# The streamed weights' pool laid out first in SBUF, the constants and x behind it

## The chip, the core and the metric

One core of a Trainium2 chip runs the whole kernel. The metric is device time in microseconds for one execution, the median of the runs; a run is one launch.

## The reference, cut to what matters

One hybrid layer on x of 256 tokens by 2048 channels. All projections come from one large matrix, then four branches are made, gated, projected and summed, and a last projection and a layer norm follow:

```python
h = einsum('bsd,de->bse', x, w_in) + b_in          # 2048 -> 18048 columns
... = split(h, ...)                                # a, b, c, d branches and merge_logits
# a: gated linear recurrence; b: dilated attention, 12 heads; c: RWKV-7 scan; d: 31-tap convolution
for n in range(4):
    mixed += sigmoid(merge[:, :, n]) * ((ys[n] * silu(gates[n])) @ w_br[n])
out = layernorm(ALPHA * x + mixed @ w_out)
```

Almost all the arithmetic is in three matrices: w_in (2048 x 18048), w_br (four of 512 x 2048) and w_out (2048 x 2048), in float32, and each is read from HBM once.

## The kernel before, in words

Every weight passes through `split` (L196 to L204): a piece of 128 partitions x 1024 float32 numbers (two k-tiles of 512 columns) is loaded into a buffer `raw`, ScalarE casts it to the rounded format into `wh`, and VectorE writes the rest, `raw - wh`, into `wl`. x is split in the same way, once, at the start, into `xh` and `xl`, which stay. A product is then three matmuls: high x high, low x high, high x low. The buffers come from the pool `wp`: four of `raw`, three of `wh`, three of `wl`, of 4096 bytes in each partition.

Three loops use the pieces:

- `channel_major` (matmul in L229) has the weights as stationary operand, 128 columns of `wh` or `wl`, and moves 256 tokens past them. The moving operand is `xh`/`xl` for w_in, and `yah`/`yal`, `ych`/`ycl`, ... (the gated branch outputs, here called y) for w_br. A piece makes 24 matmuls.
- `token_major` (matmul in L248) has the tokens as stationary operand (`xh`/`xl` for the attention's V columns of w_in, `mh`/`ml` for w_out, 128 tokens each) and moves 512 columns of `wh`/`wl` past them (256 in w_out's fourth part).
- The last 256 columns of w_out (L974) lie in `lasth`/`lastl`, which take the place of `xh`/`xl`; the stationary operand is `mh`/`ml`.

Every matmul loads a stationary operand of its own, 128 columns, while the matmul before it runs. The small stages of the branches (generators, advanced by `pump` between the pieces) lie between these loops, in a program order that the framework's scheduler sets; two of them, L366 and L406, are sums over partitions with the constant `sums` as stationary operand and `sh`/`sl` moving, 256 columns.

Pools are laid out in SBUF in the order in which they are opened. The order before is: a block of 16512 bytes that the framework holds, `cp` (the constants, x), `wp` (the streamed weights), `bp` (everything else). A tile's size is rounded up to 32 bytes. All addresses here are bytes within each partition.

Of the kernel before, what the change touches and what calls it, by code (L numbers as in the profile page):

```python
# [75 lines left out]
def tile_hybrid(  # L76
# [4 lines left out]
    S, G, PE = nc.scalar, nc.gpsimd, nc.tensor  # L81
    V = Paced(tc, nc.vector)

    cp = ctx.enter_context(tc.tile_pool(name="cp", bufs=1))
    wp = ctx.enter_context(tc.tile_pool(name="wp", bufs=1))
    bp = ctx.enter_context(tc.tile_pool(name="bp", bufs=1))
    pss = ctx.enter_context(tc.tile_pool(name="pss", bufs=4, space=PSUM))
    psb = ctx.enter_context(tc.tile_pool(name="psb", bufs=4, space=PSUM))
# [973 lines left out]
```

## Time and profile before

| | |
|---|---|
| median of three runs | 1069.24 us (1069.06 to 1070.82) |
| the profiled execution | 1071.35 us, span 1069.6 us, granted clock 0.993 |
| busy, of the span | PE 98%, PEld 94%, DVE 66%, ACT 47%, POOL 4% |
| moved by DMA | 199.14 MB, mean 186 GB/s |

PE is TensorE's matmuls, PEld its weight loads, DVE VectorE, ACT ScalarE. The end of a matmul is modelled in these records, and matmuls overlap, so the duration of one (some 280 ns) is not what one costs; the time from the start of one to the start of the next is. The chain of waits merges equal neighbours, so its pieces of "x192" with a start and a length give that time as a quotient.

### The profile page before, as it was taken

To read this page: it belongs to the slowest core of one execution; us is meant where nothing else is said; L and a number is where in the kernel's file an instruction comes from. 1 tells how busy PE (TensorE), PEld (TensorE's weight loads), DVE (VectorE), ACT (ScalarE), POOL (GpSimd) and SP (SyncE) were. 2 spreads that over 40 slices of the span, in tenths; PEclk is the share of its full clock that TensorE was granted. 3 is DMA by queue.
4 is the path that set the end of the run, shared out by engine and by line. 5 is a ranking of instruction groups with operands and counts; after the bars stand their busy time and mean duration, and the time that the engine had idled before them with its cause. 6 is when DMAs were issued, how large, how long until landed. Compare 5 with 4: busy or idle time off the path is not lost.

```text
span 1069.6 us, 20338 instructions
## 1 busy us (share of the span) xinstructions
PE 1049.8 (98%) x8547; PEld 1008.0 (94%) x8547; DVE 707.6 (66%) x999; ACT 502.7 (47%) x621; POOL 39.3 (4%) x61
## 2 busy tenths in 40 slices
PE   9999999999999999999999999999999999999994
PEld 7999999989999989999999998899999999998884
DVE  6879989889769955575444444566665555556666
ACT  3474445666544435345444443346544444444342
POOL 0100000000110020000000000000000000000003
PEclk9999999999999999999999999999999999999997
DMA  9866666555576674458766666655456666766552
GB/s 309 256 208 180 197 185 181 168 165 158 176 191 179 188 196 139 149 152 263 216 182 193 182 192 181 190 166 155 130 169 195 184 191 202 211 201 210 191 188 79
DMA packets 106765, 199.14 MB, mean 186 GB/s; under 512 B 8036, under 2 KB 17024, under 8 KB 106672
## 3 DMA queue, kind: packets, MB, share of 16 engines
q1 hardware_dynamic: 102432, 185.62, 58.5%
q0 software_dynamic: 3520, 11.09, 3.6%
q8 instruction: 67, 1.10, 0.4%
q10 hardware_dynamic: 720, 1.11, 0.3%
q14 instruction: 26, 0.21, 0.1%
HBM read 194.77 MB, written 5.39 MB: 187 GB/s over the span
## 4 chain that ended last, share of the span: by engine, by line
PE 88%; DVE 6%; DMA 2%; issue 1%; ACT 1%; POOL 0%; SPq 0%; ACTq 0%
PE ps L229 69%; PE ps L248 13%; DVE wl L67 2%; DVE xw L67 2%; DMA raw<-in_w_in 1%; DVE z L67 1%; DMA x<-scr 1%; PE psl L769 1%; PE ps L974 1%; PE po L793 0%; POOL xt L600 0%; ACT wh L202 0%; ACT z L953 0%; PE py L706 0%; PE pab L550 0%
## 5 line engine op out<-in xcount | busy, mean ns | idle before, releaser
L67 DVE TENSOR_TENSOR wl<-raw,wh 128x1024 fp32r<-128x1024 f32 (+1 forms) x343 | 418.3, 1221 | 305.4 <-ACT wh L202 302.9
L202 ACT CAST wh<-raw 128x1024 fp32r<-128x1024 f32 (+1 forms) x343 | 359.0, 1048 | 488.5 <-PE ps L229 360.7
L229 PE MATMUL ps<-xh,wh 128*128 128x256 f32 x2064 | 580.0, 282 | 0.8 <-ACT wh L202 0.8
L229 PE MATMUL ps<-xl,wh 128*128 128x256 f32 x2064 | 577.7, 281 | 0.0
L229 PE MATMUL ps<-xh,wl 128*128 128x256 f32 x2064 | 574.4, 282 | 0.9 <-DVE wl L67 0.7
L229 PEld LDWEIGHTS ps<-xh,wh 128*128 128x128 f32 x2064 | 389.5, 189 | 3.1 <-ACT wh L202 2.0
L229 PEld LDWEIGHTS ps<-xl,wh 128*128 128x128 f32 x2064 | 389.7, 189 | 0.3
L229 PEld LDWEIGHTS ps<-xh,wl 128*128 128x128 f32 x2064 | 386.4, 189 | 3.3 <-DVE wl L67 2.0
L67 DVE SCALAR_TENSOR_TENSOR acc<-cu,pkt,acc 128x256 f32<-128x256 f32 x120 | 50.7, 483 | 0.0
L248 PE MATMUL ps<-wh,ml 128*128 128x512 f32 (+1 forms) x128 | 46.3, 363 | 0.0
L248 PE MATMUL ps<-wh,mh 128*128 128x512 f32 (+1 forms) x128 | 46.3, 363 | 0.0
L248 PE MATMUL ps<-wl,mh 128*128 128x512 f32 (+1 forms) x128 | 42.3, 362 | 0.0
L248 PE MATMUL ps<-wh,xh 128*128 128x512 f32 x96 | 38.1, 396 | 0.0
L248 PE MATMUL ps<-wh,xl 128*128 128x512 f32 x96 | 37.9, 395 | 0.0
L248 PE MATMUL ps<-wl,xh 128*128 128x512 f32 x96 | 34.6, 396 | 0.0
L811 ACT ACTIVATE mg<-ps,bc 128x256 f32<-128x256 f32 x64 | 26.8, 471 | 6.7 <-PE ps L229 6.6
L248 PEld LDWEIGHTS ps<-wh,ml 128*128 128x128 f32 x128 | 24.2, 189 | 3.8
L248 PEld LDWEIGHTS ps<-wh,mh 128*128 128x128 f32 x128 | 24.2, 189 | 3.7
L248 PEld LDWEIGHTS ps<-wl,mh 128*128 128x128 f32 x128 | 24.0, 189 | 3.7
L248 PEld LDWEIGHTS ps<-wl,xh 128*128 128x128 f32 x96 | 18.0, 188 | 4.4
L248 PEld LDWEIGHTS ps<-wh,xh 128*128 128x128 f32 x96 | 18.0, 188 | 4.2
L248 PEld LDWEIGHTS ps<-wh,xl 128*128 128x128 f32 x96 | 18.0, 188 | 4.2
(310 smaller groups left out, 989.7 us busy)
## 6 DMA issues: line engine op xcount, KB each, us to landing
raw<-in_w_in SPq DMA_DIRECT2D x281, 512.0 KB, 3.8
raw<-in_w_br SPq DMA_DIRECT2D x32, 512.0 KB, 4.1
raw<-in_w_out SPq DMA_DIRECT2D x32, 512.0 KB, 4.7
fscr<-frow POOLq DMA_DIRECT2D x3, 768.0 KB, 8.3
z<-in_x POOLq DMA_DIRECT2D x4, 512.0 KB, 5.3
xs<-in_x_t SPq DMA_DIRECT2D x7, 256.0 KB, 6.2
hb<-fscr POOLq DMA_DIRECT2D x3, 512.0 KB, 5.8
lng<-in_ln_g POOLq DMA_DIRECT2D x2, 512.0 KB, 6.1
```

The costliest lines, as they stand in the source:

```text
L67: ins = f(*a, **k)
L202: S.copy(h, raw)
L229: PE.matmul(o, w[:, k, j * P : (j + 1) * P], r[:, kk, :], start=(kk == 0 and i == 0 and j % 2 == 0), stop=(kk == nk - 1 and i == 2), skip_ ...
L248: PE.matmul(ps[t][:, 0:n], a(kk, t), w[:, k, :], start=(kk == 0 and i == 0), stop=(kk == KT - 1 and i == 2),)
L769: PE.matmul(ps[:, 0:w], qt[g][:, h, q * P : (q + 1) * P], kt[g][:, h, 0:w], start=True, stop=True)
L811: S.activation(g, ps[j], AF.Sigmoid, bias=bcol(c0 + j * P))
L974: PE.matmul(ps[:, 0:T], mix(a)(k, t), w[:, k, :], start=(k == 0 and i == 0), stop=(k == KT - 1 and i == 2))
```

## The change

Two lines that open pools change places:

```diff
-    cp = ctx.enter_context(tc.tile_pool(name="cp", bufs=1))
     wp = ctx.enter_context(tc.tile_pool(name="wp", bufs=1))
+    cp = ctx.enter_context(tc.tile_pool(name="cp", bufs=1))
     bp = ctx.enter_context(tc.tile_pool(name="bp", bufs=1))
```

On all five engines the built program holds the same instructions in the same order with the same waits (8006 rows on PE, 888 on DVE, 617 on ACT, 63 on POOL, 372 on SP, buffer numbers kept); what differs is the addresses of two pools. `wp` is 40960 bytes long and goes down by 45408; `cp` goes up by 40960; `bp` stays. First addresses in the two built programs, with the remainder to 64 and to 512:

| tile | before | mod 64 | mod 512 | after | mod 64 | mod 512 |
|---|---|---|---|---|---|---|
| `raw`, first of 4 | 61920 | 32 | 480 | 16512 | 0 | 128 |
| `wh`, first of 3 | 78304 | 32 | 480 | 32896 | 0 | 128 |
| `wl`, first of 3 | 90592 | 32 | 480 | 45184 | 0 | 128 |
| `xh` (and `lasth`) | 17536 | 0 | 128 | 58496 | 0 | 128 |
| `xl` (and `lastl`) | 33920 | 0 | 128 | 74880 | 0 | 128 |
| `sums` | 53056 | 0 | 320 | 94016 | 0 | 320 |
| y (`yah`, `ych`, ...) | 216032 | 32 | 480 | 216032 | 32 | 480 |
| `mh`, `ml`, `sh`, `sl` (one each) | 140256 | 32 | 480 | 140256 | 32 | 480 |

A stationary operand is 512 bytes of such a tile in each partition and a moving one 1024 or 2048, and both start at multiples of 512 from its first address, so the remainders hold for all of them.

## Rows read from the trace of the kernel before

**Rows 1.** The page's busy times, and the granted clock in 40 slices.
```profile
PE 1049.8 (98%) x8547; PEld 1008.0 (94%) x8547; DVE 707.6 (66%) x999; ACT 502.7 (47%) x621; POOL 39.3 (4%) x61
PEclk9999999999999999999999999999999999999997
```

**Rows 2.** The page's chain of waits, by line.
```profile
PE ps L229 69%; PE ps L248 13%; DVE wl L67 2%; DVE xw L67 2%; DMA raw<-in_w_in 1%; DVE z L67 1%; DMA x<-scr 1%; PE psl L769 1%; PE ps L974 1%; PE po L793 0%; POOL xt L600 0%; ACT wh L202 0%; ACT z L953 0%; PE py L706 0%; PE pab L550 0%
```

**Rows 3.** What PE waited for longest: us in total, times, longest.
```profile
PE pp L609 <- DMA x<-scr: 2.5, 1, 2.5
```

**Rows 4.** Groups of matmuls by line and shape: count, busy us, mean ns, idle.
```profile
L229 PE MATMUL ps<-xh,wh 128*128 128x256 f32 x2064 | 580.0, 282 | 0.8 <-ACT wh L202 0.8
L229 PE MATMUL ps<-xh,wl 128*128 128x256 f32 x2064 | 574.4, 282 | 0.9 <-DVE wl L67 0.7
...
L229 PE MATMUL ps<-ych,wh 128*128 128x256 f32 x64 | 18.1, 282 | 0.0
L248 PE MATMUL ps<-wh,xh 128*128 128x512 f32 x96 | 38.1, 396 | 0.0
...
L248 PE MATMUL ps<-wh,mh 128*128 128x256 f32 x32 | 9.0, 283 | 0.0
```

**Rows 5.** L229's matmuls by stretch: us, PE busy (count), clock, DMA share, GB/s.
```profile
0.00:240.00 240.00, 224.10 (x1857) 1.00 0.69 206
240.00:480.00 240.00, 210.82 (x1708) 0.99 0.59 169
...
306.85:352.00 45.15, 45.08 (x384) 1.00 0.63 180
```

**Rows 6.** The chain's pieces in two stretches with x moving: start, us, what.
```profile
129.91 35.13 PE ps L229 x296
...
479.97 145.14 PE ps L229 x1237
```

**Rows 7.** The chain, 797 to 826 us: x moving, then y moving.
```profile
797.41 22.54 PE ps L229 x192
...
819.95 5.74 PE ps L229 x48
```

**Rows 8.** Matmuls in order of time: 1st and 11th of eleven neighbours, y moving.
```profile
850.08 0.28 PE L229 MATMUL ps<-ych,wh 128*128 128x256 f32 x1
...
851.28 0.28 PE L229 MATMUL ps<-ycl,wh 128*128 128x256 f32 x1
```

**Rows 9.** The chain in token-major stretches: x, then m stationary (512, 256), then L974.
```profile
654.96 40.13 PE ps L248 x172
...
969.81 60.29 PE ps L248 x266
...
1039.66 5.26 PE ps L248 x44
...
1044.92 4.83 PE ps L974 x41
```

**Rows 10.** Matmuls in order of time: first and last of seven neighbours, `sums` stationary.
```profile
197.28 0.28 PE L366 MATMUL psm<-sl,sums 128*128 128x256 f32 x1
...
197.98 0.28 PE L366 MATMUL psm<-sl,sums 128*128 128x256 f32 x1
```

**Rows 11.** Groups of the casts and subtractions, whole pieces, on DVE and ACT.
```profile
L67 DVE TENSOR_TENSOR wl<-raw,wh 128x1024 fp32r<-128x1024 f32 x341 | 416.9, 1224 | 304.1 <-ACT wh L202 301.7 <-PE pst L783 1.4
L67 DVE TENSOR_TENSOR lastl<-raw,lasth 128x1024 fp32r<-128x1024 f32 x4 | 4.9, 1224 | 2.0 <-ACT lasth L968 2.0
...
L202 ACT CAST wh<-raw 128x1024 fp32r<-128x1024 f32 x341 | 357.8, 1050 | 484.7 <-PE ps L229 360.7 <-PE ps L248 76.3 <-issue 15.3
L968 ACT CAST lasth<-raw 128x1024 fp32r<-128x1024 f32 x4 | 4.2, 1050 | 5.4 <-DMA raw<-in_w_out 5.4
```

**Rows 12.** The chain, 309 to 390 us, by line.
```profile
by line: DVE wl L67 28.0%; DVE xw L67 23.5%; issue 14.4%; PE ps L229 13.7%; DMA x<-scr 9.5%; POOL xt L600 5.5%; DVE gd L67 2.9%; DVE mixed L67 2.1%; DVE mg L67 1.7%; ACT wh L202 1.3%; POOL x L601 0.8%; DVE ydl L67 0.1%
```

**Rows 13.** The longest piece of the chain's start.
```profile
13.35 7.51 DMA raw<-in_w_in
```

More of the change, by code (lines that the diff above doesn't have):

```diff
@@ L82, in tile_hybrid @@
     V = Paced(tc, nc.vector)
+    wp = ctx.enter_context(tc.tile_pool(name="wp", bufs=1))
     cp = ctx.enter_context(tc.tile_pool(name="cp", bufs=1))
-    wp = ctx.enter_context(tc.tile_pool(name="wp", bufs=1))
     bp = ctx.enter_context(tc.tile_pool(name="bp", bufs=1))
```

## The prediction

> **What bounds the kernel now.** I read the page's busy times first, then the chain, then PE's own waits. PE is busy over 98% of the span, and its granted clock is full (the 2.4 GHz level) in 39 of 40 slices, 7 tenths in the last [rows 1]. The chain lies 69% on the matmuls of L229 and 13% on those of L248 [rows 2]. PE's longest wait is 2.5 us, once, near 389 us [rows 3], and its waits in L229 for `wh` and `wl` come to 0.8 and 0.7 us [rows 4]. So the time is a count of matmuls times what one costs, plus a start and an end of some 20 us. L229 has 3 x 2064 matmuls with x moving and twelve groups of 64, that is 768, with y moving; L248 has three groups of 96 with x stationary (512 columns), three of 96 with m stationary (512), three of 32 with m stationary (256) [rows 4].
>
> Since no instruction moves, only the spacing of matmuls, the speed of ACT and DVE on the moved tiles, and the loads into `raw` can change. So I look for rows in which the same form of instruction meets different addresses.
>
> **What addresses do to a matmul before.** I call *distance* the address of the moving operand less that of the stationary one, to the modulus 512. In the two token-major stretches shape and type agree, and only tiles differ: with x stationary 40.13 us / 172 = 233.3 ns each, with m stationary 60.29 / 266 = 226.7 [rows 9]. The first is distance 480 - 128 = 352, the second 480 - 480 = 0. At 256 columns with m stationary: 5.26 / 44 = 119.5 with `wh`/`wl` moving (distance 0), 4.83 / 41 = 117.8 with `lasth`/`lastl` moving (distance 128 - 480, that is 160) [rows 9]. And in L229, where stretches of x and y alternate: x moving 22.54 / 192 = 117.4 (distance 160), y moving 5.74 / 48 = 119.6 (distance 0) [rows 7]. In the steady part of a y stretch ten steps take 1.20 us, 120.0 each [rows 8]; a stretch's first matmuls are a little closer, which makes 119.6 of 120.0 in 48. Three pairs, and in each the two streams' addresses go with the spacing. I conclude that a matmul's reads and the next one's weight load disturb each other, by their addresses.
>
> Is it the distance, or each operand's own place? At L366 `sums` is stationary and `sl`/`sh` move: distance 480 - 320 = 160, but with the moving tile at 32 mod 64 and the stationary at 0, the reverse of x's pair. Six steps take 0.70 us, 117 each [rows 10], x's spacing. So two pairs at one distance, in opposite places, cost the same. I take the distance as what counts, from 8 matmuls only; this is the weakest step.
>
> The Trainium skill, SBUF — State Buffer, section Specifications (TRN2), gives lines of 16 bytes. By that, 32 and 0 mod 64 are equally whole lines, and alignment alone would change nothing; the rows agree in so far as the reverse pair costs the same.
>
> **The change, part by part.** After it `wh` and `wl` stand at 128 mod 512, as x does. Four products change their distance:
>
> - *x moving* (6192): 160 to 0. After: what y has now, 119.9 (120.0 in steady state, a little less after a break). Before: in the first 240 us 35.13 / 296 = 118.7; in the middle 45.15 / 384 = 117.6; after 480 us 145.14 / 1237 = 117.3, and 117.4 between y stretches [rows 5 to 7]. Why it is 118.7 early the trace doesn't say; I keep it. L229 has 6960 in all, 1857 before 240 us and 1708 from there to 480 [rows 5], so 3395 after; of y's sixteen stretches of 48, two lie in the first part, six in the second and eight in the third, which leaves 1761, 1420 and 3011 with x. 1761 x 1.2 + 1420 x 2.3 + 3011 x 2.5 ns = 2.1 + 3.3 + 7.5 = **+12.9 us**.
> - *y moving* (768): 0 to 352. At 256 columns no row has 352; 160 is the nearest (both are 32 mod 64), 117.4. 768 x -2.2 ns = **-1.7 us**. From the other side, the 512-column row at 352 loses 6.6 ns to distance 0, which would be +5.1 us.
> - *x stationary, 512 columns* (288): 352 to 0, so 233.3 to 226.7: **-1.9 us**.
> - *m stationary*: at 512 columns (288) 0 to 160. The only 512-column row off 0 is 352: 233.3, **+1.9 us**; if 160 helps here as it does at 256 columns (-2.2), -0.6 us. At 256 columns (96) 119.5 to 117.8: **-0.2 us**.
>
> L974 and the `sums` products keep their distances: 0.
>
> *What swallows some.* From 307 to 389 us the chain runs on DVE (51% on the subtractions and the small `xw` chain, 14% on L229) [rows 12], and PE reaches its one long wait of 2.5 us at the end of it [rows 3]. The matmuls with x moving there, 384 in the first 45 us [rows 5] and about half as many behind, get 2.3 ns longer each, 1.3 us, inside that wait: **-1.3 us**. Elsewhere PE is the chain and nothing covers it.
>
> *ACT and DVE*: the subtraction takes 1224 ns whether its other tiles stand at 32 mod 64 (`wl`) or 0 (`lastl`), the cast 1050 both ways [rows 11]. So 0; and were they slower, PE's waits for them in L229 are 1.5 us in all [rows 4].
>
> *Loads into `raw`*: no load of that size lands at 0 mod 64 before. They are on the chain at the start alone, its longest piece there 7.51 us [rows 13]; I take 0, and allow that piece a tenth either way, 0.8 us.
>
> Sum: 12.9 - 1.7 - 1.9 + 1.9 - 0.2 - 1.3 = **+9.7 us**. Against the profiled execution's own 1071.35 us (its span of 1069.6 and 1.8 around it) that is 1081.05; it lay 2.1 us over the median, so against the median 1069.24 + 9.7 = 1078.9, say **1079.0 us**, slower by 0.9%.
>
> **The rivals.**
>
> *Both operands on the grid of 64 is best (faster).* If each operand's own start counts, then 120.0 with both at 32, 117.4 with one, and by the same step 114.7 with both at 0: x moving saves 117.9 (6192 weighed as above) - 114.7 = 3.2 ns x 6192 = 19.8 us, y 1.7, and x and m stationary cancel as above: 1069 - 21.5, about 1048 us. It decides at the x spacing: under 117 it wins. For it: both-at-32 is the dearest 256-column pair, and no row has both at 0. Against it: at 512 columns moving one operand to 0 mod 64 made it dearer, 226.7 to 233.3 [rows 9]. It gets 0.15.
>
> *Nothing changes.* The Trainium skill, TensorE: Matmul & The Clock Gate, section Part 2: What happens when you issue a matmul, says of the weight load's read port that the load "doesn't steal SBUF read bandwidth from the running matmul"; by it addresses would not matter. As a mechanism of this kernel: the spacing is set by what surrounds a stretch, since x itself has 118.7 early and 117.3 late at the same addresses [rows 6], so y's 119.6 would come from its short stretches. Then x keeps its spacing: 1069 us. Against it, long stretches at L248 differ too [rows 9]. 0.13.
>
> *Slower, but by more.* Distance 352 costs y +5.1 us instead of -1.7, nothing is swallowed, x comes to 120.0 throughout (+13.5): 13.5 + 5.1 - 1.9 + 1.9 - 0.2 = 18.4 us, 1088 us. It is part of the forecast's side.
>
> **How the numbers follow.** The forecast's side (x near 120, the rival above taken in) has 0.72; its own range is 1074 to 1088: below, x at 118.7 as it already is early for half of its runs (half of 12.9 lost), above, the last rival. The measurement of this kernel can tell about 0.2% (2.1 us) from no change. No change has 0.13, faster 0.15. To hold 8 in 10 I take the range down to 1067, which takes in no change, and up to 1088; it leaves out the faster rival. Faster 0.15, same 0.13, slower 0.72.
>
> **What would show it.** In the chain after 790 us, pieces of 192 with x moving should take 23.0 us instead of 22.54, pieces of 48 with y 5.6 to 5.7 instead of 5.74; the stretch with x stationary should fall to 226.7, the one with m stationary rise towards 233. The cast and the subtraction stay at 1050 and 1224 ns, the wait of 2.5 us shrinks to some 1.2. If x's pieces of 192 take 22.0 us or less, own alignment counts, and I am wrong in sign; if they stay at 22.5, addresses are not what parts x from y.

## The result, and the profile after

The changed kernel takes 1081.72 us (median of four runs, 1080.26 to 1083.1) against 1069.95 for the kernel before, run beside it (1069.06 to 1070.82): a ratio on record of 1.0098, 95% interval 1.0079 to 1.0116 (the quotient of these two medians is a little more, 1.0110), so slower by 1.0%. Its profiled execution took 1081.0 us with a span of 1079.2. The 1081.0 us are 9.65 over the 1071.35 that the forecast's sum of +9.7 was added to; the medians lie 11.8 us apart, and the forecast was 1079.0.

The page of the changed kernel, its busy times, clock and chain by engine and by line, beside [rows 1, 2]:

```profile
PE 1060.8 (98%) x8547; PEld 1019.8 (94%) x8547; DVE 708.0 (66%) x999; ACT 502.2 (47%) x621; POOL 39.3 (4%) x61
...
PEclk9999999999999999999999999999999999999998
...
PE 97%; DVE 1%; DMA 1%; ACT 0%; SPq 0%; issue 0%; ACTq 0%
```

PE is busy for 11.0 us more with the same 8547 matmuls; DVE, ACT and POOL are where they were, within half a microsecond. The granted clock is no lower in the mean (0.994 of full speed against 0.993), so the clock is not what made it slower. The pieces of the chain of the changed kernel (start, us, what), in order: x moving early, x moving in the middle, x stationary, x moving in one piece between two of y, y moving, m stationary at 512 columns, at 256 columns, and L974:

```profile
129.83 35.28 PE ps L229 x294
...
478.97 152.04 PE ps L229 x1267
...
659.97 40.12 PE ps L248 x177
...
803.45 22.80 PE ps L229 x190
...
826.49 5.75 PE ps L229 x48
...
977.82 60.21 PE ps L248 x257
...
1049.99 4.58 PE ps L248 x39
1054.57 4.82 PE ps L974 x41
```

Divide each length by its count. x moving comes to 120.0 ns in all three pieces (before 118.7, 117.3 and 117.4 [rows 6, 7]), y to 119.8 (119.6 [rows 7]). x stationary falls to 226.7 and m stationary rises to 234.3: against [rows 9], 233.3 and 226.7, the two have changed places. x stationary now has the distance 0 that m stationary had, and m stationary has left it. At 256 columns m stationary falls from 119.5 to 117.4, and L974, whose distance stays, reads 117.6.

The casts and subtractions of the changed kernel, grouped by shape (busy us, mean ns, idle before):

```profile
L67 DVE TENSOR_TENSOR wl<-raw,wh 128x1024 fp32r<-128x1024 f32 x341 | 417.0, 1224 | 312.5 <-ACT wh L202 310.4 <-PE ps L229 0.8
...
L202 ACT CAST wh<-raw 128x1024 fp32r<-128x1024 f32 x341 | 357.4, 1049 | 498.5 <-PE ps L229 383.7 <-PE ps L248 76.5 <-issue 16.1
```

Neither has moved [rows 11]. What did move is the wait near 389 us. PE's waits after, by length (us in total, times, longest):

```profile
PE ps L229 <- ACT wh L202: 2.0, 1, 2.0
...
PE ps L229 <- DVE wl L67: 0.5, 1, 0.5
```

The wait of L609 for the load of `x` [rows 3] is gone, not shortened. With it went something that I had not read. PE's stretches around it in the kernel before (us, PE busy, granted clock, DMA share, GB/s):

```profile
389.00:392.00 3.00, 0.54 (x6) 1.00 1.00 210
392.00:394.00 2.00, 2.00 (x13) 0.64 0.61 226
394.00:396.00 2.00, 2.00 (x11) 0.51 0.08 15
396.00:398.00 2.00, 2.00 (x70) 1.00 0.85 248
```

Behind the wait the granted clock falls to half, the 1.2 GHz level, for most of 4 us. In the changed kernel PE stays busy through the same place and the clock stays full:

```profile
389.00:392.00 3.00, 3.00 (x27) 1.00 1.22 184
392.00:394.00 2.00, 2.00 (x19) 1.00 1.01 260
394.00:396.00 2.00, 2.00 (x18) 1.00 1.05 187
396.00:398.00 2.00, 2.00 (x28) 1.00 0.97 294
```

The same piece of 23 matmuls of L229 took 4.44 us there before and takes 2.94 now: in the chain of before, and below it in that of after,

```profile
392.11 4.44 PE ps L229 x23
```

```profile
394.92 2.94 PE ps L229 x23
```

The changed kernel has such a stretch too, at another place. Near 9 us PE waits 2.0 us for a cast (0.8 before [rows 4]), and behind it, the same columns, first after, then before:

```profile
12.00:14.00 2.00, 1.80 (x8) 0.50 1.07 380
14.00:16.00 2.00, 2.00 (x15) 0.74 1.11 347
```

```profile
12.00:14.00 2.00, 2.00 (x19) 1.00 1.06 373
14.00:16.00 2.00, 2.00 (x19) 1.00 1.10 345
```

### The profile page after: what moved, and what is told of

Same layout as the page of the kernel before. It is cut to its first block, busy times and chain, and to the rows that moved or that the text cites. A ratio compares the mean times of both kernels' runs of the same rounds, so it can differ in the third digit from the quotient of the medians.

```text
span 1079.2 us, 20338 instructions
## 1 busy us (share of the span) xinstructions
PE 1060.8 (98%) x8547; PEld 1019.8 (94%) x8547; DVE 708.0 (66%) x999; ACT 502.2 (47%) x621; POOL 39.3 (4%) x61
## 4 chain that ended last, share of the span: by engine, by line
PE 97%; DVE 1%; DMA 1%; ACT 0%; SPq 0%; issue 0%; ACTq 0%
PE ps L229 78%; PE ps L248 13%; DVE z L67 1%; PE psl L769 1%; DMA raw<-in_w_in 1%; PE ps L974 1%; PE po L793 0%; ACT z L953 0%; PE py L706 0%; PE pab L550 0%; PE pst L783 0%; PE pu L669 0%; PE po L795 0%; PE pst L700 0%; PE psa L690 0%; PE pswa L477 0%
## 5 line engine op out<-in xcount | busy, mean ns | idle before, releaser
L229 PE MATMUL ps<-xh,wh 128*128 128x256 f32 x2064 | 585.1, 284 | 2.0 <-ACT wh L202 2.0
L229 PE MATMUL ps<-xl,wh 128*128 128x256 f32 x2064 | 582.9, 283 | 0.0
L229 PE MATMUL ps<-xh,wl 128*128 128x256 f32 x2064 | 579.6, 284 | 0.5 <-DVE wl L67 0.5
L229 PEld LDWEIGHTS ps<-xh,wh 128*128 128x128 f32 x2064 | 396.4, 192 | 4.3 <-ACT wh L202 3.2
L229 PEld LDWEIGHTS ps<-xl,wh 128*128 128x128 f32 x2064 | 396.5, 192 | 0.3
L229 PEld LDWEIGHTS ps<-xh,wl 128*128 128x128 f32 x2064 | 393.7, 192 | 2.2 <-DVE wl L67 1.1
```

What stands on the lines that cost most here:

```text
L229: PE.matmul(o, w[:, k, j * P : (j + 1) * P], r[:, kk, :], start=(kk == 0 and i == 0 and j % 2 == 0), stop=(kk == nk - 1 and i == 2), skip_ ...
```

## The experiments

All comparisons are with the kernel before, run on the same chip; its median there was 1071.43 to 1072.72 us. A figure like 1.0008 behind a time is the ratio on record with its 95% interval; it can differ from the quotient of the medians by up to 0.2%. In the sections below "w" is `wh`/`wl`, and spacings are pieces of the chain divided by their counts, or, where it is said, means over the starts of neighbouring matmuls in the trace. The pieces quoted of e1 to e7 are those between about 481 and 600 us, with x moving, unless the text says otherwise. My theory: the distance sets the spacing, whatever the order of the pools. The rivals: each operand's own place counts; or the new place of the pools costs something else (loads into `raw`, casts).

**New order, old distances (e1).** The changed kernel with unused bytes ahead of the weights' pieces and behind them, ahead of x, so that x's distance is 160 again:

```diff
     wp = ctx.enter_context(tc.tile_pool(name="wp", bufs=1))
+    wp.tile([P, 88], F32, name="front")
     cp = ctx.enter_context(tc.tile_pool(name="cp", bufs=1))
+    cp.tile([P, 40], F32, name="tail")
```

> The pools in the new order, but 352 unused bytes ahead of the pieces and 160 behind them, so that wh and wl stand at 480 mod 512 again while x stays at 128: distance 160 as before, in the new regions of the memory. If the distance counts: pieces of 192 with x moving take 22.5 us (117.4 ns each), x stationary 233, m stationary 226.7, and the time is that of before, 1070 us (within 2 us). If it counts which pool lies first or in which region a tile lies: x stays at 120.0 ns, 1081 us.

```profile
480.88 119.21 PE ps L231 x1016
```

That is 117.3 ns, and the time is 1072.97 against 1072.72 us: 1.0008, interval 0.9992 to 1.0024. The loss is gone with the order of the pools kept.

**Old order, x moved (e2, e3).** 352 bytes ahead of `xh` and 160 behind `xl` give x the distance 0 with both operands at 32 mod 64; 192 and 320 give it 352. The edit of the first:

```diff
+    cp.tile([P, 88], F32, name="front")
     xh = cp.tile([P, KT, T], F32R, tag="xh", name="xh")
     xl = cp.tile([P, KT, T], F32R, tag="xl", name="xl")
+    cp.tile([P, 40], F32, name="tail")
```

> The pools in the old order, x moved by 352 bytes to 480 mod 512, the weights left at 480: distance 0 for x with all tiles in their old regions, and both operands at 32 mod 64 instead of at 0. If the distance counts: x moving 120.0 ns, y 119.6, x stationary 226.7, m stationary 226.7, and +12.9 - 1.9 - 2.5 = about +8.5 us, 1078 us. If regions or the order of the pools count: 117.4 ns and 1070 us.

> The pools in the old order, x moved by 192 bytes to 320 mod 512, the weights at 480: distance -160, that is 352, at which y cost 120.0 ns after the change. 160 and 352 are both 32 mod 64. If only the halves of 64 bytes count: x moving stays at 117.4 ns, 1070 us, and y's 120.0 after the change has to do with y (short stretches, or its tiles). If a wider modulus counts (128, 256 or 512): x moving 120.0 ns, and about +13 - 2.5 = +10 us, 1080 us; x stationary (distance 480 - 320 = 160) 233 or 234.

The piece in the first, then in the second:

```profile
480.90 119.16 PE ps L231 x993
```

```profile
480.94 119.16 PE ps L231 x993
```

120.0 ns in both; 1079.96 us (1.0068, 1.0046 to 1.009) and 1080.76 (1.0086, 1.0061 to 1.0112), that is 7.2 and 8.0 us more than before, where 8.5 and 10 were expected. With the first, 120.0 at distance 0 stands for x with both operands at 32 mod 64, as it does in the changed kernel with both at 0: own alignment falls as a cause. The second says it again, since there x is at 0 and the weights at 32 mod 64 as in the kernel before, and x costs 120.0 instead of 117.3. It also says that 352 is as dear as 0, so my neighbour for y's new distance, 160, was the wrong one.

**Which distances are cheap (k1, k2, k3, then k4).** `xh` and `xl` with 32 unused bytes after every two k-tiles, so that each of the eight pieces of a column group meets a distance of its own; three starting points cover all sixteen. The fourth run does it in steps of 16 bytes from 160 on. The core of the edit:

```diff
-    xh = cp.tile([P, KT, T], F32R, tag="xh", name="xh")
+    G2 = 2 * T + 8
+    xh = cp.tile([P, KT // 2, G2], F32R, tag="xh", name="xh")
```

> The pools in the old order, x laid out with 32 unused bytes after every two k-tiles, so that the eight pieces of a product meet x at distances 160, 192, ... 384, each for 24 matmuls (the zeros of the first matmuls lie in another pool to make room; weights, y and m keep their places). If the modulus is 64: spacing alternates between 117.4 (160, 224, 288, 352) and 120.0 (192, 256, 320, 384). If it is 128, 160 and 288 agree, 352 and 224 agree, 256 and 384 agree. Any distance that costs under 117 would be a better place than that of before.

> The first sweep, with everything behind x moved on by 192 bytes: the eight pieces of a product meet x at distances 480, 0, 32, 64, 96, 128, 160, 192. With a period of 256 in the distance (0 and 256 agreed at 120.0): 32 agrees with 288 (117.7), 64 with 320 (117.6), 96 with 352 (119.8), 128 with 384 (118.7), 480 with 224 (118.4); 160 and 192 repeat 117.4 and 113.6. With a period of 512 only 0, 160 and 192 are known. With 64 all would alternate.

> The same with 288 bytes: distances 384, 416, 448, 480, 0, 32, 64, 96. With a period of 256, 448 agrees with 192 (113.6) and 416 with 160 (117.4). With 512, 416 and 448 are open.

> The first sweep with steps of 16 bytes: the eight pieces of a product meet x at distances 160, 176, ... 272. 160, 192, 224 and 256 repeat 117.4, 113.6, 118.4 and 120.0. Open are 176, 208, 240 and 272; if the unit of the disturbance is 32 bytes they lie at or between their neighbours, if it is 16 bytes one of them can be under 113.3, which would be a better place.

The whole kernels took 1073.14, 1070.95, 1069.82 and 1071.54 us (one run each), since they hold cheap and dear distances together. Two pieces of the first, at distance 256 and at 192, in the chain:

```profile
504.56 2.75 PE ps L238 x23
...
521.63 2.50 PE ps L238 x22
```

119.6 and 113.6 ns, same line and shape, 17 us apart. From the starts of the 10th to the 24th matmul of a piece, over all such pieces of k1 to k3 (distances d and d + 256 together, as they agree within 0.5 ns):

| distance mod 256 | 0 | 32 | 64 | 96 | 128 | 160 | 192 | 224 |
|---|---|---|---|---|---|---|---|---|
| ns from start to start | 120.0 | 117.6 | 117.6 | 119.9 | 118.7 | 117.4 | 113.6 to 114.1 | 118.4 |

So over these distances the period is 256, not the 512 that I worked with, and it is no smooth curve: k4 reads 118.1 at 160, 119.2 at 176, 113.7 at 192, 119.5 at 208, 118.2 at 224, 117.2 at 240, 120.0 at 256, 118.5 at 272. One multiple of 16 stands out.

**x at 192 (e4), x and y at 192 (e5), the new order at 192 (e8).** e4 has the kernel before with 32 bytes ahead of `xh` and 480 behind `xl`. e5 has 32 ahead, 224 behind, and 192 ahead of the first y; e8 is the changed kernel with x and y moved to the same distance. The edit of e8, the change's two lines left out:

```diff
+    cp.tile([P, 48], F32, name="front")
     xh = cp.tile([P, KT, T], F32R, tag="xh", name="xh")
     xl = cp.tile([P, KT, T], F32R, tag="xl", name="xl")
+    cp.tile([P, 56], F32, name="tail")
...
+        if not ypad:
+            ypad.append(bp.tile([P, 48], F32, name="ypad"))
```

> The pools in the old order, 32 unused bytes ahead of x and 480 behind it: x at 160 mod 512, weights, y and m at 480 as before; distance of x 192, at which the first sweep showed 113.6 ns in its steady part. If the distance sets the spacing and PE is the bound: x 118 to some 114 ns, 6192 x -4 = -25 us, x stationary (distance 320) 230 instead of 233, -0.8 us; time about 1047 us against 1072 of before on this chip, ratio 0.976. If 113.6 was only a state between two neighbours in the sweep: x stays near 117.5, ratio 1.00. If ACT, DVE or the loads can't keep up with 2.73 us for a piece: a ratio between, with PE waiting for wh or wl.

> The pools in the old order; x moved against the weights so that its distance is 192 to the modulus 256 (32 unused bytes ahead of x, 224 behind it), and 192 unused bytes ahead of the y tiles, so that theirs is 192 too; m stationary stays at distance 0. If the modulus is 256 and y behaves as x: x as in the run with x at 160 (114.9 ns in the mean, with a part of the first 240 us at 117.8), y 113.5 to 115 instead of 119.7, 768 x -5 = -4 us on top of the -18 us there: about 1050 us against 1072, ratio 0.979. If y has a spacing of its own: 0.983.

> The pools in the new order, weights' pool first, with unused bytes that put x and y at distance 192 from the weights (192 ahead of x, 224 behind it, 192 ahead of y) and m at 0 to the modulus 256. If the distance to the modulus 256 is all that the order of the pools changed: the time of the best run so far, ratio 0.98 to before, x 113.3 in its steady part. If the new order has a cost of its own beside the distance: a ratio over that, towards 0.99.

They took 1053.84 us (0.9829, 0.9783 to 0.9874), 1052.15 (0.9816, 0.9786 to 0.9847) and 1048.53 (0.9765, 0.972 to 0.9809); e4 was expected at 1047 and e5 at 1050. An early and a middle piece of e4, then of e8:

```profile
99.98 50.06 PE ps L231 x425
...
480.92 119.11 PE ps L231 x1051
```

```profile
99.90 50.21 PE ps L231 x443
...
480.99 119.11 PE ps L231 x1051
```

In the middle both read 113.3. Early, e4 reads 117.8 where e8 reads 113.3, at one and the same distance: there are two spacings at 192. What chooses between them is not the address alone, since e4's tiles lie in the same places early and in the middle; and it is not the part of the kernel, since between 700 and 960 us e4 reads 114.0 and e8 117.5 (means over the starts with x moving). So the gain is a little less than the middle gives (mean over x's matmuls in e4 114.9, in e8 115.4). y follows too: some 115 in e5 and 117 in e8, where before it was 119.7. So does L974, another pair of tiles, with `lasth`/`lastl` in x's place moving and m stationary: 117.4 before, 120.0 in e2 and in e3, 113.7 in e4. What e8 settles is that the order of the pools costs nothing that shows: with it and the right distance the kernel is 2.3% faster than before.

**Which load does a stream meet (e6, e7).** The distance above is one number for all three products. With `xh`, `xl`, `wh`, `wl` at 160, 352, 480 and 160 mod 512 each product has its own, so that a matmul's own load, the next one's and the one after can be told apart. e7 is e6 with the products in another order:

```diff
-                    for i, (w, r) in enumerate(((h, rh), (h, rl), (l, rh))):
+                    for i, (w, r) in enumerate(((h, rh), (l, rh), (h, rl))):
```

> Which weight load does a matmul's stream meet, its own or the next one's? xh at 160, wh at 480, xl at 352, wl at 160 mod 512. A matmul with the weights that the next one loads, as they follow each other: (xh, wh) 192, (xl, wl) 192, (xh, wh) 192. With its own: (xh, wh) 192, (xl, wh) 384, (xh, wl) 0. If a stream meets the next load: 113.6 ns throughout for x, and the time some 20 us under that of before. If it meets its own: a mean of 113.6, 118.7 and 120.0, about 117.4, and the time of before.

> The addresses of the run on the next load (xh 160, wh 480, xl 352, wl 160), with the three products in another order: (xh, wh), (xh, wl), (xl, wh). Pairs of a stream with its own weights' load are unchanged: 192, 0, 384. With the next one's: (xh, wl) 0, (xh, wh) 192, (xl, wh) 384, the same three. With the one after the next: (xh, wh) 192, (xh, wh) 192, (xl, wl) 192. So if a stream meets the load after the next: 113.5 ns throughout and some 20 us off. If it meets its own: about 119 as in that run, 1075 us; the next load alone was excluded there.

The piece in e6, and in e7:

```profile
480.89 119.15 PE ps L236 x993
```

```profile
480.90 119.14 PE ps L236 x976
```

120.0 where the next load predicted 113.6 and a matmul's own load 117.4; 122.1 where the load after the next predicted 113.5 and a matmul's own about 119. The times were 1075.54 and 1082.91 us (one run each). So all three theories miss, if one load alone is to set the spacing as the table gives it. The distances to a matmul's own load are the same in both runs, and the spacings are not. Taken product by product, from the start of (`xh`, `wh`), (`xl`, `wh`) or (`xh`, `wl`) to the next start, the means between 481 and 600 us are 118.9, 119.1 and 122.0 ns in e6; in e7 they are 119.2, 126.0 and 121.1. None comes near the 113.6 of distance 192, which (`xh`, `wh`) has to its own load in both, and three are dearer than anything in the table. Several loads together are left. So is another rival: both runs also put `xl` 192 bytes from `xh` and `wl` 192 from `wh` (mod 256), which in all other runs are 0 apart. Neither was tried alone.

## Why the prediction was right, and where it was not

The forecast held in sign, in size and in its main term. Step by step, with clean means of the starts in place of the pieces where they differ:

- *The distance, and not each operand's place, from 8 matmuls of L366.* The weakest step held: 120.0 at distance 0 in three combinations of places (y before, x in e2, x after), and 117.3 at 160 in e1 with the pools in the new order.
- *x moving, +12.9.* 117.83 to 119.93 ns over 6192 matmuls: +13.0.
- *y moving, -1.7.* This failed in sign: 119.70 to 119.98, 768 matmuls, +0.2. I took 160 for the neighbour of 352, because both are 32 mod 64. The sweep shows that 352 goes with 96, at 119.9. The bound from the other side, +5.1, was much too far.
- *x stationary, -1.9*: 233.26 to 227.06, -1.8. *m stationary at 512 columns, +1.9*: 226.76 to 234.25, +2.2; *at 256, -0.2*: -0.2. What holds at 256 columns (160 cheap) did not hold at 512, so a row of the same length was the right one to take, though at another distance.
- *What the wait swallows, -1.3*: mis-sized. I let it swallow only the longer matmuls between 307 and 389 us. But PE came to the place more than 5 us late (the 3000th matmul of L229, near 384 us before, is 5.3 us later), so the whole 2.5 us went, and with it 1.5 us (4.44 - 2.94) at the lower clock behind it: -4.0. I had read the clock as full there: a 9 in [rows 1] means 90% or more of full speed, and the 0.99 of [rows 5] for 240 to 480 us held the slow stretch. Here the wait was worth its length and the slow stretch that followed it.
- *ACT and DVE, 0*: held. *Loads into `raw`, 0*: the 200th matmul of L229 is 1.7 us late, of which 0.2 is x's longer spacing and +1.5 was not in the sum. It comes from the longer wait near 9 us and the stretch at half clock behind it, shown above. The address of `raw` does not explain it: k1, where `raw` keeps its very addresses, has such a stretch (0.50 from 14 to 16 us) and is 2.1 us late; e2, where it keeps them mod 512, has one (0.62 and 0.52 from 12 to 16 us) and is 1.5 us late; and e1, with the weights' pool first, has none and is 0.3 us early. Of the fourteen profiled executions eight have a stretch at half clock between 11 and 17 us, with both orders of the pools; in the other six, the kernel before among them, the 200th matmul comes within 0.4 us of before. So these 1.5 us look like chance of one execution; what decides it is open.

The terms as measured come to 13.0 + 0.2 - 1.8 + 2.2 - 0.2 - 4.0 + 1.5 = 10.9 us against 9.6 in the spans, which leaves -1.3 us. Of these -0.8 are six matmuls of L229 between 89 and 367 us that started 0.19 to 0.36 us behind the one ahead of them before, and 0.12 us behind it now; the rest has no place. The closeness of +9.7 is in part luck, since errors cancel: y +1.9, the stationary terms and x +0.5, the start +1.5, against the wait's -2.7 and these -1.3. One more number of the forecast does not come out of its own words: half of 12.9 us lost gives a lower end of 1072.5 us, not 1074; nothing hangs on it.

Of the rivals, own alignment falls with 120.0 for x with both operands on the grid of 64. "Nothing changes" falls with e1 to e3, where nothing but addresses differ. The sentence that stood beside it, that the weight load "doesn't steal SBUF read bandwidth from the running matmul" (the Trainium skill, TensorE: Matmul & The Clock Gate, section Part 2: What happens when you issue a matmul), is not what shows here if one reads it as "addresses don't matter": the same matmul costs 113.3 to 120.0 ns by them. Whether the load is what takes the time, the runs do not show.

That a matmul's reads and the next one's weight load are what disturb each other was an argument, and it is not shown. The dependence on the distance is shown, wherever the high and low parts share one remainder; its cause is not, since the forms of it that e6 and e7 tried (the next load, the matmul's own, the one after the next) all missed.

## What to carry to other kernels

When a kernel is a long row of short matmuls, each with a weight load of its own, compare the start-to-start time of one shape over all pairs of tiles that meet in it: a spread of a few per cent that goes with the address of one operand less the other's (here mod 256) is a lever of padding, and also what a harmless-looking reorder of pools can lose. Change the order of pools or the size of a tile ahead of others only with that number in view. And when work gets longer ahead of a wait of the bounding engine, take off the whole wait as soon as the delay exceeds it (here 5.3 us against 2.5), and look in the granted clock for a slow stretch behind it.

## What the runs showed of the hardware that was not expected

- A 256-column matmul with its own weight load costs 113.3 to 120.0 ns by the distance mod 256, with one sharp minimum at 192 (176 and 208 read 119.2 and 119.5). Why 192 is not known. Where high and low parts have different remainders it costs more, 122.1 in e7.
- At one distance there are two spacings: 113.3 and 117.8 at 192 (e4), 117.3 and 118.7 at 160 before [rows 6]. They last for tens of microseconds each; in the changed kernel, at 0, the long pieces all read 120.0. What switches them is open.
- After a wait of 2.5 us in PE the granted clock was 0.64 and 0.51 in the next two stretches of 2 us; near the start of the changed kernel, behind a wait of 2.0 us, it was 0.50 from 12 to 14 us. Eight of the fourteen profiled executions had such a stretch near the start and six had not.
